# A Strassen-Winograd up projection: weight sums by accumulating transfers, 512-wide products, and mixed tiles spread over the value products

## The chip, the cores and the metric

The kernel runs on one core of one Trainium2 chip. The metric is the device time of one execution in microseconds; the kernel before took 3102.44 us (median of three runs).

## What is computed

One layer of a hybrid encoder block for 512 tokens of width 2048, all in float32. Cut to what matters here:

```python
def reference(x, mem, ...):
    h = x
    y = _rmsnorm(h, norm_mix) @ w_in
    mixed = concat([_gdn_group(y[..., :GDN_COLS]), _rwkv_group(y[..., GDN_COLS:])])
    h = h + mixed @ w_out
    h = h + _cross_attention(_rmsnorm(h, norm_xattn), _rmsnorm(mem, norm_mem), wq, wk, wv, wo)
    hn = _rmsnorm(h, norm_mlp)
    h = h + jnp.square(jax.nn.relu(hn @ mlp_w_up)) @ mlp_w_down
    return _rmsnorm(h, norm_final)
```

`mixed` is 512 x 2048, `mem` has 256 tokens, and `mlp_w_up` is 2048 x 8192. The change lies in `hn @ mlp_w_up` and in the place where `mixed` is brought back for `mixed @ w_out`.

## The kernel before

Everything is kept transposed: a tile has 128 features in its partitions and 512 tokens along it. A float32 product is made of three products of rounded parts: each operand is split into a high part (`fp32r`, a cast on ScalarE) and a low part (the rest, a subtraction on VectorE), and TensorE adds up high x high, high x low and low x high. `split` (lines 130 to 137) issues cast and subtraction; `mm` (line 124) issues a matmul; the names `whi` and `wlo` are the parts of a weight tile of 128 x 1024 that was loaded as `wraw`. There are two buffers of each (`NWS`), and three of `wraw` (`NWR`).

The first 1150 us (projections, the two recurrent groups, and parts of the attention) are ordered by a planner in the kernel. They leave `mixed` as 16 tiles in device memory (`mixd`). From line 1167 on, the framework's own scheduler orders the instructions of each engine by their dependences; the order of the code is its preference. The stages there, with the names of their PSUM tiles, are: `vp` (value products, 16 of them), `vo` (values by output weights, kept in memory as `VOd`), `op` (`mixed @ w_out`), `sc` (scores and softmax), `at` (attention output), `up` and `dn` (the MLP), and the final norm.

**The mixed tiles (lines 1187 to 1194).** Before the value products a loop over 16 tiles loads each one from `mixd` into one of the three `sl` buffers and splits it into `oh` and `ol`, which `op` needs. The `sl` buffers also serve the value products, which take one each (line 1211).

**The up stage (lines 1350 to 1416 and 1457 to 1474).** The product with `mlp_w_up` is done by the Strassen-Winograd scheme on blocks of two by two: 32 pairs of weight row tiles (index `p`), and the tokens in two halves of 256 (`HA` is columns 0 to 255, `HB` 256 to 511). For each pair there are four weight tiles `a11`, `a21`, `a22`, `a12` of 128 x 1024 (`src[0]` to `src[3]`), and seven products instead of eight. The seven combinations of activations (`B11`, `T1`, `T2`, `T3`, `T4`, `B22`, `B21`) are made once, ahead of the stage; a tile of `comb` holds a combination's 256 high columns in its `HA` half and its 256 low columns in its `HB` half. The weight combinations are made anew for each pair: `s1 = a21 + a22`, `s2 = s1 - a11`, `a21 = a11 - a21` and `s4 = a12 - s2` on GpSimd, in the two `ws` buffers and one `wraw` buffer.

`product(i, tag, a)` splits `a`, and for each of eight blocks of it issues two matmuls 256 wide with the high weights (against the high and the low columns) and later one with the low weights, all into the same 256 columns of a PSUM tile. The order of the products is B11, T1, T2, T3, T4, B22, B21. VectorE adds the results up into `c1` and `c2` (`add`, line 1381), two `sl` tiles that hold the output pair. `square` (lines 1458 to 1463) applies the norm, the ReLU and the square to each half, and ScalarE's queue stores a finished tile to `Ud`. `used` loads the first tiles for `dn` while the last pair runs.

Loads are issued by SP, whose queue is in order: a load that waits for its buffer holds back the loads behind it. GpSimd's, VectorE's and ScalarE's queues are in order, too.

Of the kernel before, what the change touches and what calls it, by code (L numbers as in the profile page):

```python
# [9 lines left out]
F32 = mybir.dt.float32  # L10
F32R = mybir.dt.float32r
AF = mybir.ActivationFunctionType
ALU = mybir.AluOpType
# [4 lines left out]
P = 128  # L18
T = 512
M = 256  # L20
KD = 16
# [52 lines left out]
def build(tc, I, out):  # L74
    nc = tc.nc
    V, S, GP, PE = nc.vector, nc.scalar, nc.gpsimd, nc.tensor
# [5 lines left out]
    pw = es.enter_context(tc.tile_pool(name="pw", bufs=1))  # L82
# [37 lines left out]
    def psb(nm, tag="mx", bufs=2):  # L120
        return tile_of(ps, [P, 512], F32, tag, nm, bufs)

    def mm(o, l, r, start=True, stop=True):
        PE.matmul(o, l, r, start=start, stop=stop)  # L124
# [14 lines left out]
    NWR, NWS, NY = 3, 2, 4  # L139
# [36 lines left out]
    def tile_of(pool, shape, dt, tag, nm, bufs):  # L176
        t = pool.tile(shape, dt, tag=tag, name=nm, bufs=bufs)
        turns[tag] = turns.get(tag, -1) + 1
        slot[t.tensor.name] = (tag, turns[tag] % bufs)
        holder[tag, turns[tag] % bufs] = t.tensor.name  # L180
        return t
# [995 lines left out]
    def sl2(w=512):  # L1177
        cnt[0] += 1
        return ph.tile([P, 512], F32, tag="sl", name=f"sl{cnt[0]}", bufs=3)[:, 0:w]

    pl_cm = tc.tile_pool(name="pl", bufs=1, reuse_waits="tile")
    pl = pl_cm.__enter__()
# [2 lines left out]
        return pl.tile([P, 512], F32R, tag="actc", name=nm, bufs=10)  # L1185

    oh, ol = [], []
    for n in range(KD):
        r = sl2()
        nc.sync.dma_start(r, mixd[n])  # L1190
        hi, lo = (ctile if n >= 12 else btile)(f"oh{n}"), (ctile if n >= 12 else btile)(f"ol{n}")
        split(r, hi, lo)
        oh.append(hi)
        ol.append(lo)
    vhi, vlo = [], []
    for n2 in range(8):
        hi, lo = act_tile(f"vhi{n2}"), act_tile(f"vlo{n2}")
        for i in range(2):
            n = 2 * n2 + i
            pt = psb(f"vp{n}", "mm", 2)  # L1200
            for h in range(2):
                wh, wl = wload(I["wv"][n][:, h * 1024:(h + 1) * 1024])
                for k in range(h * 8, h * 8 + 8):
                    sl = slice(k % 8 * P, k % 8 * P + P)
                    if k == 0:
                        mm(pt, wh[:, sl], mhl[k], start=True, stop=False)
                    mm(pt[:, 0:M], wl[:, sl], mhl[k][:, 0:M], start=False, stop=False)
                    if k > 0:
                        mm(pt, wh[:, sl], mhl[k], start=False, stop=k == KD - 1)
            h2, l2 = hi[:, i * M:(i + 1) * M], lo[:, i * M:(i + 1) * M]  # L1210
            u, t = rstd[:, M:2 * M], sl2(M)
            S.copy(u, pt[:, M:2 * M])
            V.tensor_tensor(out=t, in0=pt[:, 0:M], in1=u, op=ALU.add)
            V.tensor_tensor(out=t, in0=t, in1=mrs, op=ALU.mult)
            split(t, h2, l2)
            vhi.append(h2)
            vlo.append(l2)
    for g in range(4):
        for h in range(4):
            pts = [psb(f"vo{g}_{h}_{mt}", ("mm", "mg")[h % 2]) for mt in range(2)]  # L1220
            for q in range(2):
                wh, wl = wload(I["wo"][g, h][:, q * 1024:(q + 1) * 1024])
                for mt in range(2):
                    for e in range(2):
                        d = q * 2 + e
                        sl = slice(e * 512, e * 512 + 512)
                        vh = vhi[h * 4 + d][:, mt * P:(mt + 1) * P]
                        vl = vlo[h * 4 + d][:, mt * P:(mt + 1) * P]
                        mm(pts[mt], vh, wh[:, sl], start=(d == 0), stop=False)
                        mm(pts[mt], vh, wl[:, sl], start=False, stop=False)  # L1230
                        mm(pts[mt], vl, wh[:, sl], start=False, stop=(d == 3))
            for mt in range(2):
                ev = sl2()
                S.copy(ev, pts[mt])
                nc.scalar.dma_start(VOd[g][:, h * 2 + mt, :], ev)
# [12 lines left out]
    for n in range(KD):  # L1248
        xr = sl2()
        nc.sync.dma_start(xr, I["xT"][:, n, :])  # L1250
        pt = psb(f"op{n}", "mm", 2)
        gemm(pt, I["w_out"][n], KD, oh, ol)
        V.tensor_tensor(out=hres[n], in0=pt, in1=xr, op=ALU.add)
        hi, lo = act_tile(f"hh{n}"), act_tile(f"hl{n}")
# [17 lines left out]
    for g in range(2):  # L1272
        pts = [psb(f"sc{g}_{t}", ("mm", "mm", "mg", "mg")[t]) for t in range(4)]
        for n2 in range(8):
            cnt[0] += 1
            raw = pw.tile([P, 1024], F32, tag="wraw", name=f"kqr{cnt[0]}", bufs=NWR)
# [5 lines left out]
            for i in range(2):  # L1282
                n = 2 * n2 + i
# [8 lines left out]
        for t in range(4):  # L1292
            for e in range(2):
                s = pts[t][:, e * M:(e + 1) * M]
                mx = pl.tile([P, 1], F32, tag="mx1", name=f"mx{g}_{t}_{e}", bufs=4)
# [9 lines left out]
        for e in range(2):  # L1305
            for mt in range(2):
                pt = psb(f"ptr{g}_{e}_{mt}")
# [9 lines left out]
    HA, HB = slice(0, M), slice(M, 2 * M)  # L1317
    comb = [[None] * 8 for _ in range(7)]
# [8 lines left out]
    B11, T1, T2, T3, T4, B22, B21 = range(7)  # L1327
# [6 lines left out]
    def sub(o, a, b):  # L1334
        GP.tensor_tensor(out=o, in0=a, in1=b, op=ALU.subtract)
# [14 lines left out]
    def strassen(nm, pool, src, ks, done, used=None):  # L1350

        w = len(ks) * P

        def raw(p_, tag, bufs, i):
            cnt[0] += 1
            r = p_.tile([P, 1024], F32, tag=tag, name=f"{tag}_{cnt[0]}", bufs=bufs)[:, 0:w] \
                if p_ is pw else p_.tile([P, pool[1]], F32, tag=tag, name=f"{tag}_{cnt[0]}", bufs=bufs)[:, 0:w]
            if i is not None:  # L1360
                nc.sync.dma_start(r, src[i])
            return r

        def product(i, tag, a):
            cnt[0] += 1
            hi = pw.tile([P, 1024], F32R, tag="whi", name=f"whi{cnt[0]}", bufs=NWS)[:, 0:w]
            lo = pw.tile([P, 1024], F32R, tag="wlo", name=f"wlo{cnt[0]}", bufs=NWS)[:, 0:w]
            split(a, hi, lo)
            pt = psb(f"{nm}_{i}", tag)[:, 0:M]
            for z, k in enumerate(ks):  # L1370
                sl = slice(z * P, z * P + P)
                mm(pt, hi[:, sl], comb[i][k][:, HA], start=z == 0, stop=False)
                mm(pt, hi[:, sl], comb[i][k][:, HB], start=False, stop=False)
            for z, k in enumerate(ks):
                mm(pt, lo[:, z * P:z * P + P], comb[i][k][:, HA], start=False, stop=z == len(ks) - 1)
            if used:
                used(i)
            return pt

        def add(o, a, b, op=ALU.add):  # L1380
            V.tensor_tensor(out=o, in0=a, in1=b, op=op)

        a11 = raw(pw, "wraw", NWR, 0)
        a21 = raw(pw, "wraw", NWR, 1)
        a22 = raw(pool[0], "wraw2", 3, 2)
        a12 = raw(pool[0], "wraw2", 3, 3)
        p1 = product(B11, "mx", a11)
        c1 = sl2()
        c11, c12 = u1, u4 = c1[:, HA], c1[:, HB]
        S.copy(u1, p1)  # L1390
        s1 = raw(pool[0], "ws", 2, None)
        GP.tensor_tensor(out=s1, in0=a21, in1=a22, op=ALU.add)
        p5 = product(T1, "mg", s1)
        s2 = raw(pool[0], "ws", 2, None)
        sub(s2, s1, a11)
        p6 = product(T2, "mm", s2)
        c2 = sl2()
        c21, c22 = u3, u2 = c2[:, HA], c2[:, HB]
        add(u2, u1, p6)
        add(u4, u2, p5)  # L1400
        sub(a21, a11, a21)
        p7 = product(T3, "mm", a21)
        add(u3, u2, p7)
        add(c22, u3, p5)
        done(1, HB, c2)
        p4 = product(T4, "mx", a22)
        add(c21, u3, p4, ALU.subtract)
        done(1, HA, c2)
        s4 = raw(pool[0], "ws", 2, None)
        sub(s4, a12, s2)  # L1410
        p3 = product(B22, "mg", s4)
        add(c12, u4, p3)
        done(0, HB, c1)
        p2 = product(B21, "mm", a12)
        add(c11, u1, p2)
        done(0, HA, c1)

    acc = ph.tile([P, T], F32, tag="acc", name="acc2", bufs=1)
    alloc(range(7))
    for n in range(KD):  # L1420
        pt = psb(f"at{n}", "mm", 2)
# [35 lines left out]
    for p in range(32):  # L1457
        def square(i, half, c):
            t = c[:, half]
            V.scalar_tensor_tensor(out=t, in0=t, scalar=0.0, in1=rstd[:, half], op0=ALU.max, op1=ALU.mult)  # L1460
            S.activation(t, t, AF.Square)
            if half is HA:
                nc.scalar.dma_start(Ud[p][:, i, :], c)

        def used(i):
            if p == 0 and i == T2:
                pt = psb("pss2")
                mm(pt, ones, acc)
                rsq(rstd, pt, 1.0 / 2048, b_eps6)
            if p == 31 and i in (T1, T2, T3):  # L1470
                for f in (range(0, 3), range(3, 6), range(6, 8))[i - T1]:
                    usplit(f)

        strassen(f"up{p}", (pu, 1024), [I["w_up"][p, i] for i in range(4)], list(range(8)), square, used)
    for e in range(8):
        uh, ul = uhl[0][e * 8:], uhl[1][e * 8:]
        for n in range(KD):
            if e < 7 and n % 2 == 0:
                usplit(e * 8 + 8 + n // 2)
            pt = psb(f"dn{e}_{n}", "mm", 2)  # L1480
# [8 lines left out]
    pt = psb("pss3")  # L1489
    mm(pt, ones, acc)  # L1490
    rsq(rstd, pt, 1.0 / 2048, b_eps6)
    for n in range(KD):
        o = sl2()
# [102 lines left out]
```

## Time and profile before

| | us |
|---|---|
| median of three runs (3100.49 to 3102.53) | 3102.44 |
| the profiled execution | 3098.14 |
| its span (first to last instruction) | 3096.4 |
| TensorE busy | 3021.1 |
| VectorE busy | 1927.4 |
| ScalarE busy | 1334.0 |
| GpSimd busy | 574.9 |
| up stage in the chain of work that ended last | 642.38 |
| dn stage in the same chain | 696.36 |
| longest wait of TensorE between 1140 and 1215 | 19.85 |

Times in the rows of the profile are counted from the start of the span. In a row of a group stand the line of the code, the engine, the operation, output and inputs by name, the shapes and the count; then the busy time and the mean duration in ns; then the idle time of the engine just before these instructions and what released it. Matmuls overlap in the pipeline, so their listed durations are longer than the time from one to the next.

### The profile page before, as it was taken

The page shows a single profiled execution, that of the slowest core. Times are in us where ns is not written, and L with a number is a line of the kernel's source. Part 1 is how long each engine was busy: PE and PEld are TensorE (multiplying, and loading weights), DVE is VectorE, ACT ScalarE, POOL GpSimd, SP SyncE. Part 2 cuts the span into 40 slices and gives each one's busy share as a digit, 9 for nine tenths or more (in the row PEclk, how much of TensorE's full clock was granted, in tenths as well). Part 3 has the DMA queues.
Part 4 walks back from the last instruction along what each step waited for, and adds up shares of the span by engine and source line. Part 5 has one row for each costly group of instructions (what it writes and reads, how often), then busy time and mean ns, then how long its engine had stood idle before and what let it go on. Part 6 is the DMA issues. An engine that isn't in the chain of part 4 may idle for free.

```text
span 3096.4 us, 50566 instructions
## 1 busy us (share of the span) xinstructions
PE 3021.1 (98%) x20598; PEld 2603.5 (84%) x20598; DVE 1927.4 (62%) x2619; ACT 1334.0 (43%) x1816; POOL 574.9 (19%) x707
## 2 busy tenths in 40 slices
PE   8999999999999997999999999999999999999996
PEld 6878888888777896878887899999999888888885
DVE  6576666666667645534338899989988433444434
ACT  6455455454555554543326544444444222222222
POOL 0302312311311000000002555555552000000000
PEclk9999999999999998999999999999999999999998
DMA  5322422322424585763323344343444333333332
GB/s 173 106 86 79 107 78 82 105 84 79 136 80 149 184 275 188 230 227 124 113 89 96 116 137 132 123 134 130 131 136 167 124 111 113 123 123 126 115 96 95
DMA packets 221849, 394.73 MB, mean 127 GB/s; under 512 B 91112, under 2 KB 110828, under 8 KB 221616
## 3 DMA queue, kind: packets, MB, share of 16 engines
q1 hardware_dynamic: 207792, 366.33, 38.0%
q10 hardware_dynamic: 13824, 25.17, 2.2%
q8 instruction: 162, 2.65, 0.4%
q14 instruction: 71, 0.58, 0.1%
HBM read 343.84 MB, written 47.59 MB: 126 GB/s over the span
## 4 chain that ended last, share of the span: by engine, by line
PE 92%; DVE 2%; DMA 2%; ACT 2%; issue 1%; POOL 0%; SPq 0%; ACTq 0%; DVEq 0%; POOLq 0%
PE dn L124 22%; PE up L124 21%; PE py L248 20%; PE op L124 6%; PE kq L248 3%; PE sc L124 3%; PE vp L124 3%; PE kp L248 3%; PE vo L124 3%; PE at L124 2%; PE rs L248 1%; DMA sl<-mixd 1%; PE gs L248 1%; PE pgB L248 1%; DVE wlo L248 0%
## 5 line engine op out<-in xcount | busy, mean ns | idle before, releaser
L132 ACT CAST whi<-wraw 128x1024 fp32r<-128x1024 f32 x368 | 386.5, 1050 | 806.5 <-PE dn L124 431.1
L133 DVE TENSOR_TENSOR wlo<-wraw,whi 128x1024 fp32r<-128x1024 f32 x368 | 544.4, 1479 | 162.9 <-ACT whi L132 160.5
L124 PE MATMUL up<-cb,whi 128*128 128x256 f32 x3584 | 469.3, 284 | 4.5 <-ACT whi L132 4.5
L124 PEld LDWEIGHTS up<-cb,whi 128*128 128x128 f32 x3584 | 448.8, 193 | 5.4 <-ACT whi L132 5.3
L124 PE MATMUL dn<-uh,whi 128*128 128x512 f32 x1024 | 398.3, 389 | 0.0
L124 PE MATMUL dn<-ul,whi 128*128 128x512 f32 x1024 | 398.3, 389 | 0.0
L124 PE MATMUL dn<-uh,wlo 128*128 128x512 f32 x1024 | 398.3, 389 | 0.0
L248 PE MATMUL py<-xhi,whi 128*128 128x512 f32 x928 | 374.2, 403 | 11.6 <-ACT xhi L248 10.1
L248 PE MATMUL py<-xhi,wlo 128*128 128x512 f32 x928 | 372.2, 401 | 0.6 <-DVE wlo L248 0.5
L248 PE MATMUL py<-xlo,whi 128*128 128x512 f32 x928 | 371.9, 401 | 0.2 <-DVE xlo L248 0.2
L1482 DVE TENSOR_TENSOR h<-h,dn 128x512 f32<-128x512 f32 x128 | 88.0, 687 | 373.2 <-PE dn L124 373.2
L248 DVE TENSOR_TENSOR wlo<-wraw,whi 128x1024 fp32r<-128x1024 f32 x180 | 221.1, 1229 | 132.2 <-ACT whi L248 128.6
L248 ACT CAST whi<-wraw 128x1024 fp32r<-128x1024 f32 x180 | 188.9, 1050 | 233.7 <-PE py L248 189.9
L124 PE MATMUL up<-cb,wlo 128*128 128x256 f32 x1792 | 252.5, 284 | 1.2 <-DVE wlo L133 1.2
L124 PEld LDWEIGHTS up<-cb,wlo 128*128 128x128 f32 x1792 | 231.9, 193 | 1.5 <-DVE wlo L133 1.5
L124 PEld LDWEIGHTS dn<-uh,wlo 128*128 128x128 f32 x1024 | 192.3, 188 | 39.9
L124 PEld LDWEIGHTS dn<-uh,whi 128*128 128x128 f32 x1024 | 192.3, 188 | 39.9
L124 PEld LDWEIGHTS dn<-ul,whi 128*128 128x128 f32 x1024 | 192.3, 188 | 39.8
L248 PEld LDWEIGHTS py<-xhi,whi 128*128 128x128 f32 x928 | 175.2, 189 | 51.1 <-ACT xhi L248 10.1
L248 PEld LDWEIGHTS py<-xhi,wlo 128*128 128x128 f32 x928 | 175.0, 189 | 37.7 <-DVE wlo L248 1.7
L248 PEld LDWEIGHTS py<-xlo,whi 128*128 128x128 f32 x928 | 175.2, 189 | 34.7 <-issue 0.8
L133 DVE TENSOR_TENSOR wlo<-ws,whi 128x1024 fp32r<-128x1024 f32 x96 | 159.3, 1660 | 28.7 <-ACT whi L132 28.7
(688 smaller groups left out, 5298.4 us busy)
## 6 DMA issues: line engine op xcount, KB each, us to landing
wraw<-in_w_up SPq DMA_DIRECT2D x128, 512.0 KB, 4.0
wraw<-in_w_dn SPq DMA_DIRECT2D x128, 512.0 KB, 3.5
wraw<-in_w_in SPq DMA_DIRECT2D x118, 512.0 KB, 3.6
wraw<-in_wk SPq DMA_DIRECT2D x32, 512.0 KB, 3.7
wraw<-in_wqT SPq DMA_DIRECT2D x32, 512.0 KB, 4.1
wraw<-in_wv SPq DMA_DIRECT2D x32, 512.0 KB, 3.8
wraw<-in_wo SPq DMA_DIRECT2D x32, 512.0 KB, 3.8
wraw<-in_w_out SPq DMA_DIRECT2D x32, 512.0 KB, 3.9
```

Of the source, the lines that this page charges most:

```text
L124: PE.matmul(o, l, r, start=start, stop=stop)
L132: S.copy(hi, src)
L133: V.tensor_tensor(out=lo, in0=src, in1=hi.bitcast(F32), op=ALU.subtract)
L248: f(*a, **k)
L1482: V.tensor_tensor(out=hres[n], in0=hres[n], in1=pt, op=ALU.add)
```

## The change

It has two parts.

In the up stage, the weight sums are no longer computed on GpSimd. The weights are loaded plainly, and GpSimd issues transfers from device memory that add to the tile they land in (`plus`). One tile `sa` becomes in turn `a21 + a22`, that plus `a11`, and that plus `a12`; another, `sb`, becomes `a21 + a11`. The signs differ from before: where the old sums subtracted, the new ones add, and the signs are put right where the products are combined (`less`, and `both` with a subtraction). `a21` is loaded twice. A high-weight matmul now takes a whole tile of `comb`, high and low columns together, and is 512 wide; the low-weight matmul adds to the first half of the PSUM tile. The two halves of a product are added up when it is combined, so each step that reads a product is two additions. The order of the products is now B11, T1, T4, T2, T3, B21, B22, and the tile of output row 0 is stored when its half `HB` is done.

In the value products, the loop over mixed tiles is gone: after each of the 16 products one mixed tile is loaded and split. It has a buffer of its own, `slr`, one for all of them.

```diff
-    for n in range(KD):
-        r = sl2()
+
+    def mixed(n):
+        r = pl.tile([P, 512], F32, tag="slr", name=f"mx{n}", bufs=1)
         nc.sync.dma_start(r, mixd[n])
         hi, lo = (ctile if n >= 12 else btile)(f"oh{n}"), (ctile if n >= 12 else btile)(f"ol{n}")
         split(r, hi, lo)
...
             vhi.append(h2)
             vlo.append(l2)
+            mixed(n)
...
-            pt = psb(f"{nm}_{i}", tag)[:, 0:M]
+            pt = psb(f"{nm}_{i}", tag)
             for z, k in enumerate(ks):
-                sl = slice(z * P, z * P + P)
-                mm(pt, hi[:, sl], comb[i][k][:, HA], start=z == 0, stop=False)
-                mm(pt, hi[:, sl], comb[i][k][:, HB], start=False, stop=False)
+                mm(pt, hi[:, z * P:z * P + P], comb[i][k], start=z == 0, stop=False)
             for z, k in enumerate(ks):
-                mm(pt, lo[:, z * P:z * P + P], comb[i][k][:, HA], start=False, stop=z == len(ks) - 1)
+                mm(pt[:, HA], lo[:, z * P:z * P + P], comb[i][k][:, HA], start=False, stop=z == len(ks) - 1)
...
+        def both(o, a, p, op=ALU.add):
+            add(o, a, p[:, HA], op)
+            add(o, o, p[:, HB], op)
+
+        def less(o, p, a):
+            add(o, p[:, HA], a, ALU.subtract)
+            add(o, o, p[:, HB])
+
+        def plus(t, i):
+            nc.gpsimd.dma_start(t, src[i], accum_op=ALU.add)
+
         a11 = raw(pw, "wraw", NWR, 0)
-        a21 = raw(pw, "wraw", NWR, 1)
+        sa = raw(pool[0], "ws", 2, 1)
+        plus(sa, 2)
         a22 = raw(pool[0], "wraw2", 3, 2)
+        sb = raw(pw, "wraw", NWR, 1)
+        plus(sb, 0)
         a12 = raw(pool[0], "wraw2", 3, 3)
+        c1, c2 = sl2(), sl2()
+        c11, c12 = u1, u4 = c1[:, HA], c1[:, HB]
+        c21, c22 = u3, u2 = c2[:, HA], c2[:, HB]
         p1 = product(B11, "mx", a11)
...
-        S.copy(u1, p1)
...
+        S.copy(u1, p1[:, HA])
+        add(u1, u1, p1[:, HB])
+        p5 = product(T1, "mg", sa)
+        plus(sa, 0)
+        p4 = product(T4, "mx", a22)
+        p6 = product(T2, "mm", sa)
+        plus(sa, 3)
+        less(u2, p6, u1)
+        both(u4, u2, p5)
+        p7 = product(T3, "mm", sb)
+        both(u3, u2, p7, ALU.subtract)
+        both(c22, u3, p5)
         done(1, HB, c2)
...
+        both(c21, u3, p4, ALU.subtract)
         done(1, HA, c2)
...
+        p2 = product(B21, "mm", a12)
+        both(c11, u1, p2)
+        done(0, HA, c1)
+        p3 = product(B22, "mg", sa)
+        less(c12, p3, u4)
         done(0, HB, c1)
...
-            if half is HA:
+            if half is (HA if i else HB):
                 nc.scalar.dma_start(Ud[p][:, i, :], c)
```

More of the change, by code (lines that the diff above doesn't have):

```diff
@@ L1381, in add @@
             V.tensor_tensor(out=o, in0=a, in1=b, op=op)
+        def both(o, a, p, op=ALU.add):
[6 more added lines that the diff above has]
+            nc.gpsimd.dma_start(t, src[i], accum_op=ALU.add)
         a11 = raw(pw, "wraw", NWR, 0)
-        a21 = raw(pw, "wraw", NWR, 1)
+        sa = raw(pool[0], "ws", 2, 1)
+        plus(sa, 2)
         a22 = raw(pool[0], "wraw2", 3, 2)
+        sb = raw(pw, "wraw", NWR, 1)
+        plus(sb, 0)
         a12 = raw(pool[0], "wraw2", 3, 3)
+        c1, c2 = sl2(), sl2()
+        c11, c12 = u1, u4 = c1[:, HA], c1[:, HB]
+        c21, c22 = u3, u2 = c2[:, HA], c2[:, HB]
         p1 = product(B11, "mx", a11)
[L1388 to L1404, printed above, removed]
+        S.copy(u1, p1[:, HA])
[10 more added lines that the diff above has]
+        both(c22, u3, p5)
         done(1, HB, c2)
-        p4 = product(T4, "mx", a22)
-        add(c21, u3, p4, ALU.subtract)
+        both(c21, u3, p4, ALU.subtract)
         done(1, HA, c2)
[L1409 to L1412, printed above, removed]
+        p2 = product(B21, "mm", a12)
[3 more added lines that the diff above has]
+        less(c12, p3, u4)
         done(0, HB, c1)
-        p2 = product(B21, "mm", a12)
-        add(c11, u1, p2)
-        done(0, HA, c1)
     acc = ph.tile([P, T], F32, tag="acc", name="acc2", bufs=1)
```

## The prediction

> **What bounds the kernel now.** I began with the page: the engines' busy shares, then the chain of work that ended last.
>
> ```profile
> span 3096.4 us, 50566 instructions
> PE 3021.1 (98%) x20598; PEld 2603.5 (84%) x20598; DVE 1927.4 (62%) x2619; ACT 1334.0 (43%) x1816; POOL 574.9 (19%) x707
> PE 92%; DVE 2%; DMA 2%; ACT 2%; issue 1%; POOL 0%; SPq 0%; ACTq 0%; DVEq 0%; POOLq 0%
> ```
>
> TensorE ends the chain for 92% of the span, so time is won by issuing less matmul time or by closing gaps in it. The change touches two places. The first is the up stage, which the chain in order of time shows as one unbroken piece, with the dn stage behind it:
>
> ```profile
> 1733.14 642.38 PE up L124 x5336
> 2375.51 696.36 PE dn L124 x3072
> ```
>
> No wait of TensorE lies in those 642 us. The windows view of 600 us of it (PE, PEld, DVE, ACT, POOL busy, then clock, DMA share, GB/s) and its groups say how near the others are:
>
> ```profile
> 1760.00:2360.00 600.00, 600.00 (x5003) 600.00 (x5002) 546.28 (x538) 267.60 (x359) 317.84 (x119) 1.00 0.41 131
> ```
> ```profile
> L133 DVE TENSOR_TENSOR wlo<-wraw,whi 128x1024 fp32r<-128x1024 f32 x119 | 236.2, 1985 | 11.6 <-ACT whi L132 11.2
> L133 DVE TENSOR_TENSOR wlo<-ws,whi 128x1024 fp32r<-128x1024 f32 x90 | 150.4, 1671 | 27.5 <-ACT whi L132 27.5
> L132 ACT CAST whi<-ws 128x1024 fp32r<-128x1024 f32 x90 | 94.4, 1049 | 105.3 <-PE up L124 100.3 <-ACT sl L1461 5.0
> L1381 DVE TENSOR_TENSOR sl<-sl,up 128x256 f32<-128x256 f32 x209 | 83.7, 409 | 13.6 <-PE up L124 13.6
> L1392 POOL TENSOR_TENSOR ws<-wraw,wraw 128x1024 f32<-128x1024 f32 x29 | 75.2, 2594 | 36.8 <-DVE wlo L133 30.4 <-DMA wraw<-in_w_up 6.3
> ```
>
> VectorE is 91% busy (546 of 600), the second limit. The second place is the start of the value products (vp). TensorE's own timeline there, and windows with the granted clock:
>
> ```profile
> 1167.11 0.40 PE L124 MATMUL vp<-mhl,whi 128*128 128x512 f32 x1
> 1187.36 0.77 PE L124 MATMUL vp<-mhl,whi 128*128 128x512 f32 x1 [19.85 <-ACT oh L132]
> 1188.35 0.63 PE L124 MATMUL vp<-mhl,whi 128*128 128x512 f32 x1
> 1188.99 0.63 PE L124 MATMUL vp<-mhl,whi 128*128 128x512 f32 x1
> 1190.91 0.49 PE L124 MATMUL vp<-mhl,whi 128*128 128x512 f32 x1
> ```
> ```profile
> 1164.00:1166.00 2.00, 2.00 (x12) 1.59 (x12) 0.38 (x2) 0.62 (x1) 0.00 (x0) 1.00 1.04 411
> 1168.00:1170.00 2.00, 0.00 (x0) 0.00 (x0) 2.00 (x3) 1.05 (x2) 0.00 (x0) 1.00 0.89 280
> 1170.00:1172.00 2.00, 0.00 (x0) 0.00 (x0) 1.89 (x3) 1.24 (x2) 0.00 (x0) 0.66 0.77 238
> 1195.00:1270.00 75.00, 75.00 (x416) 63.01 (x415) 47.29 (x65) 36.10 (x52) 0.00 (x0) 1.00 0.54 182
> ```
>
> Sixteen mixed tiles go through three buffers in a row, and the vp products stand behind them on ScalarE for 19.85 us; the clock falls to half meanwhile.
>
> **The mixed tiles.** Now one tile follows each vp product. The 19.85 us go, and so does the cold restart: from 1187.36 to 1190.91 the timeline lists five wide (512) and six narrow (256) matmuls in 3.55 us; at the prices worked out below (226.7 and 119.5 ns) they take 1.85, so 1.70 is saved. What moves into vp, for each of its products (75 us hold 416 records of 32 a product, 5.8 us each):
>
> ```profile
> 1167.49 0.61 ACT L132 CAST oh<-sl 128x512 fp32r<-128x512 f32 x1
> ```
> ```profile
> 1168.76 0.68 DVE L133 TENSOR_TENSOR ol<-sl,oh 128x512 fp32r<-128x512 f32 x1
> ```
> ```profile
> sl<-mixd SPq DMA_DIRECT2D x16, 256.0 KB, 3.3
> ```
>
> That is 0.61 us on ScalarE and 0.68 on VectorE, where 5.8 us hold 2.8 and 3.7 of work (36.10 and 47.29 of 75), and 45 GB/s beside 182. All fits. The one buffer for the tile makes load, cast and subtraction a chain of 3.3 + 0.6 + 0.7 = 4.6 us, inside 5.8. The cover is thin only if SP's queue holds the load back behind a weight load that waits for its buffer, since a cast that waits has the next weight cast behind it on ScalarE. I allow 1 us in all: -20.5 us. The bounds are -21.5 and none, the latter if every tile held TensorE up for 1.3 us.
>
> **Wide products.** Up has 32 row pairs of 7 products of 24 matmuls, 5376 (the trace lacks 40 records): 642.38 / 5376 = 119.5 ns each, 256 wide. In dn a 512-wide one takes 696.36 / 3072 = 226.7 ns. Eight pairs of each product become eight wide ones: 2 x 119.5 - 226.7 = 12.3 ns by 1792, which is -22.0 us. A product goes from 2.87 to 2.77 us, a row pair from 20.07 to 19.38.
>
> The Trainium skill ("TensorE: Matmul & The Clock Gate", section "Wait — 56ns, not 53.3ns?") puts the fixed cost of a matmul at about 2.5 ns, from which I estimate 4.5 us for this step. The trace's 12.3 ns disagrees, and I take the trace.
>
> **VectorE.** Each product now lies in two halves, so the 7 additions of a row pair become 15: 8 x 0.41 = 3.3 us more. But the sums leave GpSimd, and the subtractions run in two kinds, beside a GpSimd sum or without one:
>
> ```profile
> 2099.19 3.10 DVE L133 TENSOR_TENSOR wlo<-wraw,whi 128x1024 fp32r<-128x1024 f32 x1 [0.52 <-ACT whi L132]
> 2114.05 1.22 DVE L133 TENSOR_TENSOR wlo<-ws,whi 128x1024 fp32r<-128x1024 f32 x1
> 2115.19 0.42 DVE L1460 SCALAR_TENSOR_TENSOR sl<-sl,rstd 128x256 f32<-128x256 f32 x1
> ```
> ```profile
> 2098.80 2.40 POOL L1392 TENSOR_TENSOR ws<-wraw,wraw 128x1024 f32<-128x1024 f32 x1 [1.22 <-DVE wlo L133]
> ```
>
> With the short kind throughout, a row pair costs 7 x 1.22 + 15 x 0.41 + 4 x 0.42 = 16.4 us of 19.38, less than today's 18.3 (546.28 x 20.07 / 600). Off the path: nothing.
>
> **The accumulating transfers.** This is the unknown: no such transfer is in this trace. Per row pair there are five plain loads instead of four (a21 is loaded twice) and four accumulations of 512 KB issued on GpSimd. The sum `sa` is one buffer that changes in place: +a22, product T1, +a11, product T2, +a12, product B22. Two steps wait for readers. The tight one is +a11: it may start when T1's split has been read, and T2's cast needs it, with only the product T4 between. Behind that wait on GpSimd's queue stand +a12 and the next pair's two sums, which nothing needs for 8 us or more. From the timelines of TensorE and ScalarE, where the copy L1390 marks the end of the pair's first product:
>
> ```profile
> 2116.15 2.08 PE L124 MATMUL up<-cb,whi 128*128 128x256 f32 x16
> ```
> ```profile
> 2116.72 0.35 ACT L1390 COPY sl<-up 128x256 f32<-128x256 f32 x1
> ```
>
> T1's product starts at 2116.15, its subtraction ends at 2114.05 + 1.22 = 2115.27. T2 starts two products later, +5.54, so at 2121.69; its cast takes 1.05. Less the 0.25 that I allow for two handovers, the transfer has 2121.69 - 1.05 - 2115.27 - 0.25 = 5.1 us. What a transfer takes here:
>
> ```profile
> q1 hardware_dynamic: 17136, 62.40, 33.2%
> q10 hardware_dynamic: 8569, 15.62, 6.8%
> wraw<-in_w_up SPq DMA_DIRECT2D x116, 512.0 KB, 4.1
> ```
>
> A plain load lands in 4.1 us and keeps the 16 engines for 0.332 x 600 / 116 = 1.7 us. Bounds for the accumulation: 4.1 us (the addition is free, no stall) and 8.2 (two loads one after the other, 3.1 us of stall). I take 5.8: a load and the engine time of one more read, since the target is read too. It is nearer to the plain load, as the fixed part is paid once. That leaves TensorE waiting 0.7 us per pair, 32 x 0.7 = +22.4 us. A gain cannot come from it, TensorE having no wait here to lose. A wait this short keeps the clock: above, it still stood at 1.00 up to three microseconds into the idle time.
>
> **Sum.** -22.0 - 20.5 + 22.4 = -20 us. The profiled execution took 3098.14 us (1.7 around its span), the median is 3102.44, 4.3 more: 3078 on the first scale, 3082 on the second. A measurement of this kernel tells apart about 0.2%, 6 us.
>
> **Rivals.** First, *the late accumulation*: the same wait, longer. GpSimd's issue is unpriced, and the next pair's sums may lie in front in the same queue. The gains, 42.5 us, are used up at 1.3 us of wait per pair, so it decides from a landing time of 6.4 us, and is slower by over 0.2% from 6.6. At 8.2 us: 3102.4 - 42.5 + 99 = 3159. For it: ScalarE's cast has no other work to wait behind, so every 0.1 us costs 3.2 us. Against it: the DMA share is only 0.41, and the tight step has T4 beside it.
>
> Second, *the DMA engines fill up*. If an accumulation keeps them for two loads, a pair needs (5 + 2 x 4) x 1.72 + 1.36 for its stores (0.068 x 600 / 30) = 23.7 us, over TensorE's 19.4. That is 3.6 us over today's 20.07, x 32 = +116, less 20.5 for the mixed tiles: 3198. Against it: shares are not capacity; at 1164 the engines moved 411 GB/s at a share of 1.04, and the pair's 14 load equivalents (13 loads and 512 KB of stores, 7.34 MB) at that rate are 17.9 us, under 19.4. It makes the kernel slower if the rate for such traffic stays under 354 GB/s (7.34 MB in 20.07 + 20.5 / 32 us). The Trainium skill ("Collectives: The Full Stack", section "The bandwidth ceiling: the fold count and why AG ≠ RS ≠ AR") says that an addition in the DMA engines needs two source reads on one ring and runs at half a copy's rate, which is this rival's condition; no run here shows it.
>
> Third, *the mixed tiles still block*: the single buffer makes ScalarE wait in each vp product, and the second bound above holds. Then -22.0 + 22.4, no change, 3103.
>
> **How the numbers follow.** The forecast, a landing up to 6.2 us, has 0.51, from 3060 (no stall, 3059.9) to 3096. The late accumulation has 0.24, 3109 to 3165; the filled engines 0.16, 3165 to 3200 and beyond; the third, with landings around break-even, 0.09, of which 0.03 fall on the faster side. Faster 0.54, same 0.06, slower 0.40. The range 3058 to 3175 leaves out most of the filled engines and a few of the rest, some 0.2; the likeliest case's own range is 3060 to 3096.
>
> **What would show it.** Right: the gap at 1167 is gone and the clock stays at 1.00 through vp; wide up matmuls come every 227 ns; subtractions in up take 1.22 us; GpSimd shows no TENSOR_TENSOR there; ScalarE's cast of `ws` waits for the DMA about 0.7 us once per pair, and TensorE with it. Wrong: that wait at 2 us or more (first rival), a DMA share near 1 with plain loads also landing late (second), waits of ScalarE for the mixed loads in vp (third). An up stage of 32 x 19.4 = 620 us means that the accumulations were free.

## The result, and the profile after

The changed kernel takes 3315.64 us, the median of four runs (3310.36 to 3321.71), beside 3101.47 for the kernel before: 1.0691 times as long, with a 95% interval of 1.0672 to 1.0711. The forecast was 3082, its range ended at 3175: wrong in sign and far outside. The profiled execution took 3317.21 us. Its page, engines first, then the chain by engine:

```profile
span 3315.4 us, 47461 instructions
PE 3078.1 (93%) x18806; PEld 2562.3 (77%) x18806; DVE 1822.6 (55%) x2875; ACT 1332.6 (40%) x1816; POOL 339.9 (10%) x707
PE 51%; DMA 13%; DVE 6%; ACT 3%; issue 2%; POOL 0%; ACTq 0%; SPq 0%; DVEq 0%; POOLq 0%
```

TensorE ended 92% of the chain and now ends 51%. Transfers, VectorE and ScalarE have taken its place. Its first matmul in each stage places the loss. Vp begins at 1159.1 (before: 1155.9) and lasts 94.7 us where it lasted 114.4, so 19.6 are won. Up begins at 1702.7 and lasts 883.5 us where it lasted 656.2: 227 lost. About 8 more are lost at the start of dn, where two waits of 1.68 and 3.50 us and the clock at half follow the last pair; 3 were gone before vp, where the code is the same. The stages between are unchanged.

**Vp** looks as forecast. The windows view (columns as before) and the groups and issues of the mixed tiles:

```profile
1195.00:1250.00 55.00, 54.01 (x298) 44.77 (x297) 39.33 (x57) 29.92 (x47) 0.00 (x0) 1.00 0.72 222
```
```profile
L133 DVE TENSOR_TENSOR ol<-mx,oh 128x512 fp32r<-128x512 f32 x15 | 10.3, 685 | 0.0
L132 ACT CAST oh<-mx 128x512 fp32r<-128x512 f32 x15 | 9.3, 620 | 20.2 <-DMA mx<-mixd 20.2
```
```profile
mx<-mixd SPq DMA_DIRECT2D x16, 256.0 KB, 3.7
```

The gap of 19.85 us is gone and the clock is at 1.00. ScalarE does wait for the tiles, 20.2 us in all, but TensorE is idle for only 0.99 us of these 55.

**Up.** The windows view, and the groups of the stretch from 1760 to 2500:

```profile
1760.00:2500.00 740.00, 590.63 (x3011) 509.99 (x3010) 404.43 (x701) 243.09 (x323) 92.83 (x108) 0.87 0.77 192
```
```profile
L124 PE MATMUL up<-cb,whi 128*128 128x512 f32 x1507 | 427.0, 430 | 148.6 <-ACT whi L132 148.6
L133 DVE TENSOR_TENSOR wlo<-ws,whi 128x1024 fp32r<-128x1024 f32 x81 | 98.9, 1221 | 244.5 <-ACT whi L132 244.4
L1385 DVE TENSOR_TENSOR sl<-sl,up 128x256 f32<-128x256 f32 x351 | 141.4, 417 | 16.7 <-ACT sl L1409 10.4 <-PE up L124 1.9
L132 ACT CAST whi<-ws 128x1024 fp32r<-128x1024 f32 x81 | 84.8, 1048 | 312.4 <-DMA ws<-in_w_up 157.7 <-DMA ud<-sl 109.6 <-PE up L124 28.9
```

GpSimd issued 108 accumulations in it, four to a pair: 27 pairs, 27.4 us each where 19.4 were forecast. TensorE stood idle for 148.6 us, 5.5 a pair, always for a cast. Its busy time, 590.63 / 27 = 21.9, is 2.5 us over 19.4, and that is the clock of 0.87. ScalarE waited for the transfer into `ws`; the 109.6 us put down to stores (`ud<-sl`) are the same wait, in pairs where a store landed last by the records. VectorE is at 55%, its subtractions at 1.22 us. One pair in the timeline of the engines (T1's cast is in the first row):

```profile
2123.90 1.05 ACT L132 CAST whi<-ws 128x1024 fp32r<-128x1024 f32 x1 [0.76 <-PE up L124]
2124.61 2.00 PE L124 MATMUL up<-cb,whi 128*128 128x512 f32 x8
2125.08 0.86 POOL L1396 DMA_DIRECT2D ws<-in_w_up  x1 [11.98 <-DMA ws<-in_w_up]
2125.74 1.22 DVE L133 TENSOR_TENSOR wlo<-ws,whi 128x1024 fp32r<-128x1024 f32 x1
2127.25 0.86 POOL L1396 DMA_DIRECT2D ws<-in_w_up  x1 [1.31 <-DVE wlo L133]
2127.41 2.00 PE L124 MATMUL up<-cb,whi 128*128 128x512 f32 x8
2130.20 2.00 PE L124 MATMUL up<-cb,whi 128*128 128x512 f32 x8
2137.06 1.04 ACT L132 CAST whi<-ws 128x1024 fp32r<-128x1024 f32 x1 [7.85 <-DMA ud<-sl]
2138.16 3.78 PE L124 MATMUL up<-cb,whi 128*128 128x512 f32 x8 [5.01 <-ACT whi L132]
```

T1's subtraction ends at 2126.96, and the tight +a11 goes out at 2127.25. Two microseconds ahead of it, at 2125.08, GpSimd had issued another sum: +a22 of the next pair. T1 and T4 run, then TensorE waits 5.01 us for T2, and T2's eight wide matmuls take 3.78 us where the others take 2.00: half the clock. The issues of that instant, and the one of +a12 at 2139.66, which has nothing in front of it (KB each, us to landing):

```profile
ws<-in_w_up POOLq DMA_DIRECT2D x1, 512.0 KB, 9.7
```
```profile
ws<-in_w_up POOLq DMA_DIRECT2D x1, 512.0 KB, 6.0
```

And the queues and issues of the whole stretch (q0 holds what GpSimd issued; MB, share of 16 engines):

```profile
q0 software_dynamic: 15472, 56.30, 40.9%
q1 hardware_dynamic: 19440, 70.79, 30.0%
q10 hardware_dynamic: 7776, 14.16, 5.3%
...
wraw<-in_w_up SPq DMA_DIRECT2D x107, 512.0 KB, 5.7
ws<-in_w_up POOLq DMA_DIRECT2D x81, 512.0 KB, 7.6
ws<-in_w_up SPq DMA_DIRECT2D x27, 512.0 KB, 3.7
...
wraw<-in_w_up POOLq DMA_DIRECT2D x27, 512.0 KB, 9.3
```

An accumulation keeps the engines for 0.409 x 740 / 108 = 2.80 us, a load for 0.300 x 740 / 134 = 1.66, the stores of a pair for 1.45. That is 4 x 2.80 + 5 x 1.66 + 1.45 = 20.95 us a pair, more than TensorE's 19.4, though the engines are not full in the pair of 27.4 (a share of 0.77).

### The profile page after: what moved, and what is told of

The parts are those of the page before. It is cut to its first block, busy times and chain, and to the rows that moved or that the text cites. A ratio compares the mean times of both kernels' runs of the same rounds, so it can differ in the third digit from the quotient of the medians.

```text
span 3315.4 us, 47461 instructions
## 1 busy us (share of the span) xinstructions
PE 3078.1 (93%) x18806; PEld 2562.3 (77%) x18806; DVE 1822.6 (55%) x2875; ACT 1332.6 (40%) x1816; POOL 339.9 (10%) x707
## 4 chain that ended last, share of the span: by engine, by line
PE 51%; DMA 13%; DVE 6%; ACT 3%; issue 2%; POOL 0%; ACTq 0%; SPq 0%; DVEq 0%; POOLq 0%
PE dn L124 21%; DMA ws<-in_w_up 8%; PE up L124 7%; PE op L124 5%; DMA ud<-sl 3%; PE py L248 3%; PE sc L124 3%; PE kp L248 3%; PE vo L124 2%; PE kq L248 2%; DVE wlo L133 2%; DVE sl L1385 2%; ACT whi L132 2%; PE at L124 1%; PE vp L124 1%
## 5 line engine op out<-in xcount | busy, mean ns | idle before, releaser
L124 PE MATMUL up<-cb,whi 128*128 128x512 f32 x1792 | 506.8, 430 | 178.6 <-ACT whi L132 178.5
L124 PEld LDWEIGHTS up<-cb,whi 128*128 128x128 f32 x1792 | 358.7, 210 | 254.0 <-ACT whi L132 185.8
L133 DVE TENSOR_TENSOR wlo<-wraw,whi 128x1024 fp32r<-128x1024 f32 x368 | 450.1, 1223 | 131.8 <-ACT whi L132 130.9
L248 DVE TENSOR_TENSOR wlo<-wraw,whi 128x1024 fp32r<-128x1024 f32 x180 | 222.4, 1235 | 133.8 <-ACT whi L248 130.7
L124 PEld LDWEIGHTS up<-cb,wlo 128*128 128x128 f32 x1792 | 262.3, 203 | 22.6 <-DVE wlo L133 2.0
L133 DVE TENSOR_TENSOR wlo<-ws,whi 128x1024 fp32r<-128x1024 f32 x96 | 117.3, 1221 | 289.9 <-ACT whi L132 289.9
L124 PE MATMUL up<-cb,wlo 128*128 128x256 f32 x1792 | 265.2, 294 | 0.9 <-DVE wlo L133 0.9
L132 ACT CAST whi<-ws 128x1024 fp32r<-128x1024 f32 x96 | 100.6, 1047 | 366.0 <-DMA ws<-in_w_up 188.2
```

The costliest lines, as they stand in the source:

```text
L132: S.copy(hi, src)
L133: V.tensor_tensor(out=lo, in0=src, in1=hi.bitcast(F32), op=ALU.subtract)
L248: f(*a, **k)
```

## The experiments

Each was timed beside the kernel before on the same chip. Its ratio is to that.

**One part alone.** First the mixed tiles without the change in up (`+ mixed(n)` in the loop of the value products, up as before).

> The kernel before with the mixed tiles spread over the value products, the up stage as before. In the profile after, the vp stage went from 114.4 us (1155.9 to 1270.2) to 94.7 (1159.1 to 1253.8), so 19.6 us less than 3101.5: 3082 us, and no single wait of TensorE over 2 us between 1140 and 1280. Rival: part of that gain was only borrowed from a later stage and comes back in vo or op; then 3090 or more.

3080.53 us, 0.9934 [0.9919, 0.9948]. The mixed tiles bring 20.5 us by this ratio (21.2 between the medians), and this kernel beats both others. Of the 19.85 us of idle time 0.3 are left in vp, most of them in this window:

```profile
1166.00:1176.00 10.00, 9.77 (x56) 8.18 (x55) 6.76 (x11) 5.77 (x10) 0.00 (x0) 1.00 0.62 202
```

Then the whole change with the four sums on GpSimd as before, and no accumulating transfer.

```diff
-        plus(sa, 2)            # and the three others
+        gsum(sa, a21, a22)     # GP.tensor_tensor, into ws and wraw buffers
```

> The whole change but for the transfers: the four sums are computed on GpSimd from plainly loaded tiles, with the new signs, and the wide products and the new order stay. Theory (VectorE becomes the bound): before, VectorE was busy 18.3 us per row pair of which 13.1 were its work at undisturbed durations (7 x 1.22 + 7 x 0.41 + 4 x 0.42), so four GpSimd sums cost it 5.2; with 15 additions 16.4 + 5.2 = 21.6 us per pair, over TensorE's 19.4, and the time is 3101.5 - 19.6 + 32 x (21.6 - 20.07) = 3131 us. Rival (the wide products are free, and all of the loss is the transfers): 3060 us.

3113.3 us, 1.0036 [1.0023, 1.0049]. Of the 235 us by which the changed kernel is behind e1, 202 go with the accumulations. But the wide products gain nothing either; its window:

```profile
1760.00:2300.00 540.00, 523.09 (x2900) 442.65 (x2899) 490.94 (x673) 228.75 (x309) 293.93 (x104) 1.00 0.38 126
```

104 sums are 26 pairs, 20.8 us each, with VectorE at 91%: 18.9 us a pair, not the 21.6 expected, and still under the 19.4 that TensorE was to need. So VectorE is not full. But TensorE waits 25 times, once a pair, for a subtraction, up to 0.5 us. Two kernels have only the four independent products wide (B11, T4, B21, B22; 11 additions): e9 in the new order, e13 on e1 in the old order.

> The kernel with all sums on GpSimd (3113 us), but only four of the seven products are wide (B11, T4, B21, B22, with one more addition each); T1, T2 and T3 stay 256 wide. Theory (VectorE's extra additions cost the 33 us by which that kernel is behind the one with the mixed tiles alone): VectorE falls from 18.9 to 17.2 us per pair, TensorE takes 20.07 - 4 x 0.098 = 19.68, no waits, and the time is 3080.5 - 12.5 = 3068 us. Rival (the new order of the products costs, not the additions): still 3100 us or more.

> The kernel before with the mixed tiles spread (3080.5 us), its order of products and its sums on GpSimd, and four products wide (B11, T4, B21, B22). VectorE goes from 18.3 to 19.9 us per pair, TensorE from 20.07 to 19.68. If VectorE's order leaves no waits as with all products narrow: 3080.5 - 12.5 = 3068 us. Rival (beside GpSimd's sums any longer VectorE chain makes TensorE wait for a subtraction, as with the new order, 1.14 us per pair): 3100 us or more.

e9 3115.85, 1.0044 [1.0029, 1.0059]; e13 3120.9, 1.0066 [1.0054, 1.0079]: both as the rival had it. The wait in e9 (us in total, times, longest), then the window and the same wait of e13:

```profile
PE up L124 <- DVE wlo L133: 28.8, 25, 1.4
```

```profile
1760.00:2300.00 540.00, 517.95 (x3427) 462.14 (x3426) 524.85 (x553) 225.32 (x303) 263.12 (x101) 1.00 0.36 123
```
```profile
PE up L124 <- DVE wlo L133: 22.1, 75, 0.7
```

VectorE is busy for 97% of the window of e13, and TensorE waits 75 times for a subtraction, in e9 once a pair. Neither fewer additions nor the old order helps: in all three kernels with wide products beside GpSimd's sums, a subtraction comes too late. Which of the added operations delays it stays open.

**Addition or transfer.** The changed kernel with the four transfers as plain copies.

```diff
-            nc.gpsimd.dma_start(t, src[i], accum_op=ALU.add)
+            nc.gpsimd.dma_start(t, src[i])
```

> The changed kernel with the same 128 transfers from GpSimd's queue as plain copies instead of accumulating ones, in the same places and with the same waits; the sums of weights are left out (each tile holds the last weight copied). Theory (the price of accumulating): a copy keeps the engines 1.66 us instead of 2.8 and lands alone in some 5 us instead of 6.0, second in a row in 6.7 instead of 9.7; TensorE waits some 1.6 us per pair with the clock at 1.00, and the time is 3060 + 51 = 3111 us. Rival (the queue of GpSimd is slow whatever it carries): landings of 9 us or more and over 3250 us.

3130.51 us, 1.0086 [1.0063, 1.0109]: 19 us over the theory's 3111, far from the rival's 3250. Same queue, order and waits; 185 of the 214 us go. The page of the stretch from 1760 to 2360, with 114 copies in it:

```profile
q0 software_dynamic: 16643, 60.62, 28.7%
...
ws<-in_w_up POOLq DMA_DIRECT2D x85, 512.0 KB, 5.3
```
```profile
PE up L124 <- ACT whi L132: 34.7, 30, 3.9
```

A copy keeps the engines for 0.287 x 600 / 114 = 1.51 us and lands in 5.3 where the accumulations took 7.6. An accumulation is 2.80 / 1.51 = 1.86 copies. The Trainium skill ("Collectives: The Full Stack", section "The bandwidth ceiling: the fold count and why AG ≠ RS ≠ AR") tells of ring collectives that the addition in the DMA engines takes two source reads, at half a copy's rate; the 1.86 comes near it, for transfers that are no collective.

**The order in the queue.** Two kernels take one sum off the queue: e3 lets GpSimd compute a21 + a22, so that nothing stands ahead of the tight one; e4 lets it compute the tight one itself.

```diff
-        plus(sa, 2)
+        gsum(sa, sa, a22)      # e3; in e4 plus(sa, 0) becomes gsum(sa, sa, a11)
```

> As the changed kernel, but the first step of each sum (a21 + a22) is computed on GpSimd from the two loaded tiles; the other three steps stay transfers. So nothing stands before the tight transfer in GpSimd's DMA queue. Theory (queue order): the tight transfer lands in 6.0 us as the lone ones do at 2112 and 2139 in the profile after, against 5.1 that it has; ScalarE waits about 0.9 us per pair, the clock stays at 1.00, and the time is 3101.5 - 19.6 - 22 + 32 x 0.9 = 3089 us. Rival (an accumulating transfer is slow by itself under this load, whatever stands before it): it still lands in 9 us or more, ScalarE waits 4 us or more per pair, and the time stays above 3220 us.

> As the changed kernel, but the tight step (adding a11 between T1 and T2) is computed on GpSimd in place; the other three steps stay transfers. Theory (the tight step's landing is the whole loss): 2.4 us on GpSimd fit into the 5.1 that it has, VectorE has 16.4 + 1.3 = 17.7 us of 19.4, and the time is 3101.5 - 19.6 - 22 = 3060 us, up to 3075 if the adding of a12, which has some 8 us, waits behind the next pair's first step. Rival (the DMA engines are full: an accumulation keeps them 40.9% x 740 / 108 = 2.8 us, a load 1.66, a pair's stores 1.45): three accumulations, five loads and the stores are 18.2 us of 19.4, so loads come late and the time is over 3100 us.

3282.67 us (1.0583 [1.0563, 1.0603]) and 3308.9 (1.0669 [1.0646, 1.0693]): far over the times of both theories (3089 and 3060), and among those of the rivals. But e3's rival had the wrong cause: the tight sum landed in 5.3 us, as the theory of the queue said. Beside the GpSimd sum T1's subtraction was late, and with it the issue. In e4 the wait moved to the next sum (us in total, times, longest):

```profile
ACT whi L132 <- DMA ws<-in_w_up: 212.8, 22, 10.8
POOL wraw L1396 <- DMA wraw<-in_w_up: 102.9, 21, 5.4
```

GpSimd stands about 5 us before the sum for T3 while its plain load lands (second row), and +a12 behind it lands late for B22: ScalarE's 22 waits are one a pair. e8, with two sums on GpSimd and two as transfers, came to 3154.3 us, 1.0166 [1.0149, 1.0183], with both troubles at once: 17.8 us of VectorE a pair, and casts that wait for `ws`.

> Wide products and mixed tiles as in the changed kernel; a21 + a22 and a21 + a11 are made by accumulating transfers ahead of use, the two later sums (+ a11, + a12) on GpSimd into tiles of their own. No accumulating transfer waits for a reader. Theory (what hurts is a transfer between two products): no wait of TensorE over 1 us in a pair, VectorE at 16.4 + 2 x 1.3 = 19.0 of 19.4 us; 3060 to 3080 us. Rival (accumulating transfers and VectorE's sharing with GpSimd both cost, wherever they stand): over 3100 us, as with all sums on GpSimd (3113) or more.

e12 leaves +a22 out, which takes away one accumulation and what stands ahead of the tight one.

> The changed kernel without the first step (+ a22) of each sum, which is left out: 96 transfers, nothing before the tight one in GpSimd's queue, and no work added on GpSimd or VectorE. Queue order and full engines both say faster here (18.2 us of DMA per pair): the tight transfer lands in 6.0 us, and the time is 3089 us, up to 3110 where + a12 waits behind the step of the other sum. Rival (GpSimd's queue is too slow for an accumulation between two products in any order): over 3200 us.

3232.14 us, 1.0424 [1.0405, 1.0444], a time of the rival's. The share of the engines fell to 0.74, and yet it is slower than e10 below, which has all four. The tight sum landed in 5.6 us, but T2 still waits 2.1 us in the mean of the pairs, and B22 1.3: +a12 stands behind the sum for T3 and lands after 7.8. e5, where all four transfers run and no product reads a sum, was to give the capacity alone.

> All transfers of the changed kernel stay, but the four products that used a sum take a plainly loaded tile instead (a22 for T1 and T2, a12 for T3 and B22), so no product waits for an accumulating transfer; the values of up are other ones. Theory (single waits, not capacity): the pair runs at TensorE's 19.4 us and the time is 3101.5 - 19.6 - 22 = 3060 us. Rival (the DMA engines are full: 4 x 2.8 + 5 x 1.66 + 1.45 = 21.0 us per pair): loads come late and the time is 3060 + 32 x 1.6 = 3111 us or more.

3258.82 us, 1.0504 [1.0483, 1.0525], and it answers nothing: the scheduler put the unread sum off, its buffer held plain loads back, and TensorE stood in bursts of up to 20.7 us.

Then the four sums issued in the order of the code (e10), and with B11 moved behind T4 as well, so that two products lie between the tight sum and its reader (e11).

```diff
+            d = nc.gpsimd.dma_start(t, src[i], accum_op=ALU.add)
+            tc.keep_in_program_order(d)
```

> The changed kernel with one thing changed: GpSimd issues the accumulating transfers in the order of the code, so the tight one (+ a11) and the next (+ a12) stand before the next pair's first steps instead of behind one of them. Theory (queue order): the tight transfer lands in the 6.0 us of a lone one, waits fall to about 0.9 us per pair, and the time is 3060 + 29 = 3089 us. Rival (the DMA engines are full): by the rows of the changed kernel an accumulation keeps them 2.80 us, a load 1.66 and a pair's stores 1.45, in sum 20.95 us; then the pair cannot get under 21 us and the time is 3060 + 32 x 1.6 = 3111 us or more, with the waits moved to the transfers that now stand behind.

> As the one before, and the product B11 moved behind T4, so that two products lie between T1 and T2 and the tight transfer has 7.9 us. Queue order: no wait is left and the time is 3060 us. DMA engines full: 3111 us or more, no better than the one before, since the same bytes go through in the same order.

3196.29 us (1.0312 [1.0296, 1.0328]) and 3176.37 (1.0242 [1.0228, 1.0256]). So the scheduler's order and the missing product cost 139 of the 214 us, and still both expectations of a gain fell; the times are over the 3111 that full engines were to give at least. T1, the tight sum and T2 in e10's timeline:

```profile
2091.79 1.22 DVE L133 TENSOR_TENSOR wlo<-ws,whi 128x1024 fp32r<-128x1024 f32 x1
2092.31 2.00 PE L124 MATMUL up<-cb,whi 128*128 128x512 f32 x8
2093.30 0.86 POOL L1396 DMA_DIRECT2D ws<-in_w_up  x1 [12.22 <-DVE wlo L133]
...
2099.03 1.04 ACT L132 CAST whi<-ws 128x1024 fp32r<-128x1024 f32 x1 [4.58 <-DMA ud<-sl]
2100.11 1.23 DVE L133 TENSOR_TENSOR wlo<-ws,whi 128x1024 fp32r<-128x1024 f32 x1 [4.97 <-ACT whi L132]
2100.13 2.14 PE L124 MATMUL up<-cb,whi 128*128 128x512 f32 x8 [2.07 <-ACT whi L132]
```

The tight sum, alone now, landed in 5.7 us. But T1's subtraction ends at 2093.01, 0.7 us after T1's product has begun, where the forecast had it end 0.9 before. Of the 5.1 us 3.6 are left (2092.31 + 5.58 - 1.05 - 0.25 - 2093.01), and TensorE waits 2.07. After this wait T2's matmuls take 2.14: the clock held.

**Queue or engines.** Why does e11 still lose 75 us? Either its four sums form a chain through one queue (split, landing, split, landing), or nearly full engines make every landing late. e14 takes two plain loads out of e11 (T4 reads a11, B21 reads T3's sum). e15 leaves the load and issues the next pair's first sum right behind +a11. e16 does both.

> This is e11 (sums issued in the code's order, two products between the tight sum and its reader) with two of its four plain loads of each pair left out: T4 takes the tile of a11, B21 takes the tile of the sum of T3, and a22 and a12 are no longer loaded by themselves. Part of the computation is changed by that: two of the seven products get other weights. The four accumulating transfers, their order and every wait between them stay. Engines full: e11's accumulations at 2.93 us of the 16 engines and loads at 1.40 to 1.66 make some 20 us a pair, and 3 us of it go; e11's pair of 22.8 us falls by that to about 19.5 to 20, the time to 3080 to 3100. Serial chain (the four sums go one after another through the one queue, each with its landing of 6 to 9 us, and the share of the engines does not set it): the pair stays at 22 us or more, the time at 3150 to 3180.

> This is e11 with the next pair's two first sums made ahead: the next a21 is loaded at the start of the pair, its +a22 stands on GpSimd right behind +a11 and before +a12, and the next sum of T3 (a21 + a11) stands behind +a12. Every transfer of e11 is kept, eight of 512 KB a pair, the computation as well; only the order in the queue is another, so that +a22 no longer lands second behind +a12 after T2's split and just ahead of the next T1. Serial chain: the time between two sums of T1 has no landing on it any more, the tight +a11 has two products (5.7 us) against its lone 6.0, and the pair comes to 19.4 to 20.2 us; 3060 to 3095. Engines full: nothing goes, the pair stays at 22 to 23 us, 3150 to 3180.

> e15 and e14 together (two of the seven products get other weights, as in e14). If only the chain counts, the same as e15, within 10 us. If only the engines count, the same as e14. If both do (the chain first, the engines' load lengthening each landing), this one alone comes near 3060 and lies at least 15 us under both.

Windows of e11, e14 and e15, each with its median landing of `ws`:

```profile
1760.00:2360.00 600.00, 538.61 (x2944) 463.88 (x2943) 396.54 (x683) 230.28 (x316) 92.22 (x105) 0.98 0.89 231
...
ws<-in_w_up POOLq DMA_DIRECT2D x79, 512.0 KB, 7.5
```
```profile
1760.00:2360.00 600.00, 582.56 (x3237) 498.00 (x3237) 431.88 (x750) 254.81 (x346) 100.89 (x115) 1.00 0.83 202
...
ws<-in_w_up POOLq DMA_DIRECT2D x86, 512.0 KB, 5.6
```
```profile
1760.00:2360.00 600.00, 554.73 (x3045) 473.08 (x3044) 408.83 (x713) 239.09 (x327) 94.73 (x109) 0.99 0.89 239
...
ws<-in_w_up POOLq DMA_DIRECT2D x82, 512.0 KB, 6.9
```

e14 took 3115.01 us (1.0054 [1.0036, 1.0072]), 61 under e11 and between the two forecasts: a pair went from 600 / 26.25 = 22.9 us to 600 / 28.75 = 20.9. So the engines' load counts. It does not lengthen every landing alike, though. After T2's split GpSimd issues three sums in a row: +a12, the next pair's +a22 and its sum for T3. In one pair of e11, from 2116.28 on, the time from issue to landing (last column) was

```profile
ws<-in_w_up POOLq DMA_DIRECT2D x1, 512.0 KB, 5.5
```
```profile
ws<-in_w_up POOLq DMA_DIRECT2D x1, 512.0 KB, 9.0
```
```profile
wraw<-in_w_up POOLq DMA_DIRECT2D x1, 512.0 KB, 12.3
```

The medians of the whole stretch are 5.4, 9.2 and 12.5 us in e11, and 5.4, 8.1 and 11.6 in e14. The first sum, with nothing in front, gains nothing; those that stand behind others do. The tight sum gains most, from 7.6 to 5.4: in e11 it goes out 0.9 us before the sum for T3 has landed, in e14 at about that time. And in e11 a chain fills the pair: the tight sum lands (7.5 us, in the mean), T2 is split (2.7), +a22 goes out second (0.6) and lands (9.3), T1 is split (2.9), and the next tight sum goes out. That is 23 us, the whole pair, and hardly any of it is slack: cast and subtraction alone are 2.3 of each split.

e15 takes the landing of +a22 out of this chain. It took 3151.72 (1.0165 [1.0150, 1.0181]), 25 under e11, a time that the theory of the engines had: the order counts, but less. Neither theory alone gives both numbers. e16, at 3131.87 (1.0098 [1.0081, 1.0115]), is 17 us over e14, where its expectation had it under both: with the next sum early, T1's product waits 0.7 us for its subtraction in every pair, 20 us in 28 pairs. How the rest divides between queue and engines stays open. No order that was tried makes the accumulations pay.

## Why the prediction was wrong, step by step

- *Mixed tiles*, -20.5: right. e1 measured 20.5 alone (by its ratio), the stage 19.6 in the changed kernel.
- *Wide products*, -22.0: nearly right on TensorE. From 2124.61 to 2127.41 one product takes 2.80 us, forecast 2.77, before 2.87: 0.07 of the 0.10, some 16 of the 22 us. The Trainium skill ("TensorE: Matmul & The Clock Gate", section "Wait — 56ns, not 53.3ns?"), with its 2.5 ns, would have given an estimated 2.85.
- *VectorE, off the path*: right in the changed kernel, where GpSimd computes nothing: 1.22 us a subtraction, 404.43 / 27 = 15.0 us a pair where 16.4 were forecast. Where GpSimd does compute, TensorE waits for VectorE (e2, at 18.9 us a pair), and the gain is gone. In no run did the wide products pay without the transfers.
- *The accumulating transfers*, +22.4: this term failed, and with it the sum. It was sized at 0.7 us a pair and measured 5.5, with 2.5 more for the clock. By the pair shown above: the landing was 9.7 us instead of 5.8, and the room 4.7 instead of 5.1 (2127.41 + 5.58 - 1.05 - 0.25 - 2126.96); 9.7 + 0.3 for the issue, less 4.7, is about 5. The price of a lone accumulation, 5.8, had been right (5.7 and 6.0), but it was applied to a queue in which the accumulation is not alone. "Behind that wait stand +a12 and the next pair's two sums" was the order of the code. The scheduler put +a22 of the next pair in front.
- *The clock stays at 1.00*: this hung on a short wait. At 2.07 us it held (e10), at 5.01 it fell to half. The Trainium skill ("TensorE: Matmul & The Clock Gate", section "What's actually happening") has the clock drop after an idle window of about 3.4 us, and both rows agree.
- *Rivals.* The late accumulation named the cause, "the next pair's sums may lie in front", but its upper end was 8.2 us from two loads in a row; two accumulations in a row gave 9.7, and no cold clock was priced. The filled engines were set aside by a rate of 411 GB/s taken from plain loads. Accumulations take 2.80 us of the engines against 3.44 in that rival and 1.51 for a copy here: 20.95 us a pair, still over TensorE's 19.4. Both rivals had a part in the loss (e10 and e11 for the queue, e14 for the engines), and the prediction never had them act together.

## What to carry to other kernels

Before an engine's work is handed to accumulating transfers, count them as nearly two copies each in the budget of the DMA engines, and price the landing by what stands ahead in the same queue in the order that the scheduler will write, not in that of the code. A buffer that is updated in place between two readers is a chain with a landing in it; here the engine that computed the sums before cost less, even with two products between the sum and its reader (3113.3 us in e2, 3176.37 in e11). Where two parts are independent, time them alone: here the small one (0.9934) was the whole gain.

## What the runs showed of the hardware that was not expected

- A plain copy of 512 KB by GpSimd's queue keeps the 16 engines for 1.51 us and an accumulating one for 2.80 (the changed kernel) to 3.14 (e8, 0.283 x 600 / 54).
- What an accumulation takes to land goes by its place in the queue more than by the mean share of the engines. In the kernels in code order (e10, e11, e14; shares of 0.86, 0.89 and 0.83) the first of three took 5.4 to 5.9 us, the second 8.1 to 10.2, the third 11.6 to 13.6, in medians. At the lower share of 0.77 the changed kernel's `ws` took 7.6.
- Issuing an accumulation occupies GpSimd for 0.86 us, a plain copy for 0.53 (60.18 / 114 in e6). In the kernel before, a subtraction of 128 x 1024 on VectorE takes 1.22 us alone and up to 3.47 beside a GpSimd addition (2.4 to 3.3 us), while the additions that read a product from PSUM keep to 0.40 to 0.42. In e2 GpSimd is busy for 54% (293.93 of 540), and VectorE for 18.9 us a pair, against 15.0 in the changed kernel.
